# Three of the four mLSTM heads' output projections as Strassen's seven products, spread over the next head

## The chip, the cores and the metric

The kernel runs on one core of a Trainium2 chip. A core has five engines that run side by side and wait for one another by semaphores: TensorE (PE in the profile; PEld is its loading of the stationary operand) multiplies into the eight banks of PSUM, VectorE (DVE) and ScalarE (ACT) work elementwise on SBUF and PSUM, GpSimd (POOL) does small work and issues some DMAs, SyncE (SP) issues the loads of the weights. Each engine takes its instructions in the order of the program. The metric is the device time of one execution in microseconds.

## The reference, cut to what matters

Two layers on a sequence of 512 tokens of width 1024. Each layer is a feed-forward, a mixer, a second feed-forward and a gated embedding. The first layer's mixer is an mLSTM with four heads; its last step takes the four heads' outputs, each 512 tokens by 512, side by side and multiplies them by `ml_w_out` (2048 by 1024):

```python
proj = x @ w_in + b_in                      # q, k: 256 columns a head; v, z: 512 a head
qk = jax.nn.silu(causal_depthwise_conv(qk, conv_w))
h = mlstm_cell(q, k, v, ig, fg)             # scores, mixing, normalisation by den
h = (h - mu) * lax.rsqrt(var + LN_EPS) * norm_g
h = (h * jax.nn.sigmoid(z)).astype(x.dtype)
return h @ w_out                            # a sum over heads of h_head @ w_out[512 rows]
```

Around it stands `x = layer_norm(ALPHA * x + mix)`. So each head's 512 by 512 output times its 512 rows of `w_out` is added into the residual x.

## The kernel before, in words

**Products.** Every matmul is done three times (`mm3`): an operand is split into a high part `hi` and a low part `lo = a - hi`, and hi·hi, hi·lo and lo·hi are added up in one PSUM bank. High parts are ScalarE copies (line 193 for weights, 273 for activations), low parts VectorE subtractions (199, 274). For some weights (`low="dma"`, lines 194 to 197) ScalarE writes the negated copy and a DMA issued by POOL adds the raw weight to it.

**Weights.** `Weights` holds one list, `W.order`, of all weight tiles of the program in the order of their use. `fill` goes down this list: it loads raw tiles through SP (three buffers of 1 MB) and splits one tile whenever a split buffer of the tile's kind is free; in the mLSTM four are "main" and two "extra". `take` hands TensorE the next split tile; `release` frees its buffer and at once calls `fill`, whose copies stand in the queues of ScalarE and VectorE at that point of the program. A release with `later=True` is kept back until `refill`. So a released tile is followed by the filling of the tile six places further on, and that fill waits until TensorE has used the released one.

**Strassen in the feed-forwards.** `forms` (line 92) gives, for four 2x2 blocks of a weight, the seven weight forms of Strassen's product (the variant with shared sums); the third and the fourth (`t2`, `t1`) need two VectorE additions each, made in place in the raw tiles. Low parts of forms are always made by VectorE (`in_place`). `Group` (line 719) does the other side: `form` makes the next of seven activation forms (VectorE additions before the third, fifth and sixth, then a split), `product` multiplies it into a pair of PSUM banks, `add` adds the result of the last product into x, two 512-column VectorE adds (`residual`). The products use two pairs of banks in turn, and most accumulate on what the pair holds, so a product must wait until the add of the product two before it has read that pair. The four banks, all of "dn", are pinned from the first two products until the adds of the last two.

**PSUM.** Four "up" banks go round in a fixed order. The four "dn" banks go by `dn_order`: `dn_bank` takes the first that isn't pinned and puts it at the end.

**The mLSTM, head by head.** `project_qk` projects two q and two k blocks (24 matmuls of 512 columns each, "qps"); after each, ScalarE copies the bank to `pad` (946), VectorE does the four taps of the convolution (948, 950), and one block later ScalarE and VectorE apply the silu and split it. `project_v` does four blocks of tokens ("vps"), each split after a VectorE add (981). `scores` does four triangular blocks ("sps"); `project_z` two blocks ("zps": sigmoid on ScalarE, a scale on VectorE); `mix` the four blocks of tokens from the last to the first ("nps", with statistics on VectorE, 1049 to 1061); then two more z blocks. Then `down` multiplies the output of the head *before* by its rows of `w_out` ("dps": 4 token blocks, 4 row blocks, 2 halves), and `gate_turn` turns this head's output by transposes ("hps"), gates it and splits it into hh and hl. After the last head its own `down` follows, with the layer norm. In the last head the transposes lie between the token blocks of `down`.

The order of all of this is written out by hand in the order of the calls.

Of the kernel before, what the change touches and what calls it, by code (L numbers as in the profile page):

```python
# [9 lines left out]
F32 = mybir.dt.float32  # L10
# [36 lines left out]
class Weights:  # L47
# [179 lines left out]
                self.free[kind] += 1  # L227
            self.fill(low=low)

    def refill(self, n=1):  # L230
        for kind in self.held[:n]:
            self.free[kind] += 1
        del self.held[:n]
        self.fill()


@with_exitstack
def hybrid_trunk(ctx: ExitStack, tc, x, p, ln_g, ln_b, ffn1_wgu, ffn1_wd, ffn2_wgu, ffn2_wd,
# [93 lines left out]
    def ffn_weights(wgu, wd, name, ple=False):  # L332
# [26 lines left out]
            W.add_hook("rows", lambda hi, lo: turn_p.pop()(hi, lo))  # L359
        add_rows(wd, starts[LAST], 4, ["rows", "rows", "main", "main"] if ple else ["main", "rows", "rows", "rows"])  # L360

    def stage_kinds(first):

        n = len(W.order) - first
        for i in range(n):
            extra = i % 6 >= 4 if i < n // 6 * 6 else i >= n - 2
            W.order[first + i] = ("extra" if extra else "main",) + W.order[first + i][1:]

    def ml_weights():
        win, wout = ml_w_in[0], ml_w_out[0]  # L370
        first = len(W.order)

        def o_w(h):
            add_rows(wout, 4 * h, 4)

        for h in range(HEADS):
            W.add((w_cols(win, h * DQK), cols2))
# [10 lines left out]
        for i, kind in zip(range(-8, -4), ("extra", "extra", "main", "main")):  # L388
            W.order[i] = (kind,) + W.order[i][1:]

    def gm_weights():
# [211 lines left out]
        if norm.deferred:  # L603
            affine.extend([lambda t=t: norm.finish(t) for t in range(TB)])

    def down(hs, first, norm=None, low=(None,) * 4, between=None, lazy=False, defer=False):


        n = len(hs)
# [2 lines left out]
        def release(k):  # L612
            kind = "rows" if kinds[k] == "rows" else None
            if norm is None:
                W.release(kind=kind, low=low[k])
            elif kind == "rows":
                W.free[kind] += 1
            elif defer:
                W.release()
            else:  # L620
                W.release(later=lazy or bool(W.held))
                if not W.held:
                    W.held.append("none")

        for t in range(TB):
# [26 lines left out]
            def finish(t=t, banks=banks):  # L652
                for half, ps in enumerate(banks):
                    residual(t, half, ps, first)
                    if norm is not None:
                        norm.stats(t, half, 2)
                if between is not None:
                    between(t)
# [60 lines left out]
    class Group:  # L719
# [56 lines left out]

    def ffn(layer, k, rows, prepare=None):
# [60 lines left out]

    def mlstm():
        b_in = ml_b_in  # L840
        with stage_pool("extra", EXTRA) as extra, stage_pool("ml_parts") as near, stage_pool("ml") as mp:
            W.open("extra", extra, EXTRA)
            rows_d = dram.tile([HEADS, SEQ], F32, name="rows_d")

# [83 lines left out]
            def project_qk(h):  # L928

                qh, ql = big("A", F32R, "qh"), big("B", F32R, "ql")  # L930

# [9 lines left out]
                for i in range(4):  # L941
# [26 lines left out]
                late()  # L968
                return qh, ql

            def project_v(h, vb, between=()):
# [5 lines left out]
                for t in range(TB):  # L977
                    ps = dn_bank("vps")
                    up_tokens(t, ws, ps, release=lambda: None)
# [4 lines left out]
                    if t < len(between) and between[t]:  # L984
                        between[t]()
                return vh, vl

            def project_z(h, sz, i):

                ps = up_bank("zps")  # L990
                up(ps, W.take())
                sca.activation(sz[:, i], ps, AF.Sigmoid, bias=col("b_z", h * 4 + i))
                vec.tensor_scalar(sz[:, i], sz[:, i], col("norm_g", h * 4 + i), None, op0=OP.mult)
                W.release(later=i < 2, low="dma")
                run_affine()

            def row_tile():
                return mp.tile([P, SEQ], F32, name="rbc", tag="rbc")
# [5 lines left out]
            def scores(h, qk, rt):  # L1004
# [2 lines left out]
                res = []  # L1007
                for j in range(TB):
                    n = SEQ - j * P
                    ps = (dn_bank if j % 2 else up_bank)("sps")  # L1010
# [15 lines left out]
                    res.append((sh, sl))  # L1026
                return res

            def mix(h, ss, v):
                vh, vl = v  # L1030
                hn = big("A", F32, "hn")
                for t in reversed(range(TB)):
                    bank = up_bank if t >= 2 else dn_bank
# [30 lines left out]

            def gate_turn(h, hn, sz):

                if h < HEADS - 1:
                    hh, hl = big("hh", F32R, "hh"), big("hl", F32R, "hl")
                else:

                    hh, hl = (near.tile([P, 4, SEQ], F32R, name=n, tag=g) for n, g in (("hh", "vh"), ("hl", "vl")))

                def turn(t):
                    ps = (dn_bank if t % 2 and h < HEADS - 1 else up_bank)("hps").rearrange("p (k c) -> p k c", k=4)
# [3 lines left out]
                    hf = tmp_tile("hzf").rearrange("p (k c) -> p k c", k=4)  # L1078
                    vec.tensor_mul(hf, ps, sz[:, :, s])
                    split(hh[:, :, s], hl[:, :, s], hf)  # L1080
                return [(hh[:, i], hl[:, i]) for i in range(4)], turn

            prev = None
            for h in range(HEADS):
                vb = mp.tile([P, DV], F32, name="vb", tag="sh0")
                sca.dma_start(vb, row_ap(b_in, 2 * QK + h * DV, DV))
                if h:
                    rt = row_tile()
                    load_row(rt, h)
                qk = project_qk(h)  # L1090
                if h == 0:
                    rt = row_tile()
                    v = project_v(h, vb, (None, lambda: (gate_sums(), run_affine()),
                                          lambda: (gate_rows(), load_row(rt, h), run_affine())))
                else:
                    v = project_v(h, vb)
                W.release()
                ss = scores(h, qk, rt)
                sz = big("B", F32, "sz")
                W.release()  # L1100
                W.release(2, later=True)
                for i in range(2):
                    project_z(h, sz, i)
                hn = mix(h, ss, v)
                W.refill(4)
                for i in range(2, 4):
                    project_z(h, sz, i)
                last = h == HEADS - 1
                if last:
                    hs, turn = gate_turn(h, hn, sz)  # L1110
                if prev is not None:
                    down(prev, h == 1, low=[None, None, "dma", "dma"] if last else ["dma"] * 4,
                         between=turn if last else None)
                else:
                    norm = Norm(0, 1)
                if not last:
# [297 lines left out]
```

## Time and profile before

| | |
|---|---|
| median of 3 runs | 2244.51 us (2244.25 to 2244.77) |
| the profiled execution | 2244.37 us, its span 2242.7 us |
| TensorE busy | 2228.5 us, 99% |
| VectorE, ScalarE, POOL busy | 1482.4, 902.0, 102.8 us |
| TensorE's granted clock, mean | 0.999 |
| matmuls of 128x512 in the mLSTM's `down` (dps<-hh) | 384, of them 96 a head |

The span runs from the first to the last instruction. A matmul's row shows its whole passage (some 390 ns), while the next one starts after 227 to 233 ns; so the pace is read from starts. Numbers in brackets at the end of a timeline row are the idle time of the engine before it and what ended it. The mLSTM stands from about 362 to 776 us, its heads start at about 362, 449, 550 and 650.

### The profile page before, as it was taken

How to read it: one execution, taken by the hardware profiler on the slowest of the kernel's cores; microseconds unless marked ns; L12 is line 12 of the kernel's file. 1: busy time of each engine (PE TensorE's matmuls, PEld its weight loads, DVE VectorE, ACT ScalarE, POOL GpSimd, SP SyncE). 2: the span in 40 equal slices, each digit the busy share in tenths (PEclk: the TensorE clock that was granted, in tenths of full speed). 3: DMA queues.
4: the chain of work that ended last, by engine and by line, in shares of the span. 5: the costliest groups of instructions: out<-in, count | busy, mean ns of one | idle time of the engine just before them, and what ended most of it. 6: DMA issues, size and time to landing. Idle time of an engine off the chain costs nothing.

```text
span 2242.7 us, 26516 instructions
## 1 busy us (share of the span) xinstructions
PE 2228.5 (99%) x10625; PEld 1869.4 (83%) x10625; DVE 1482.4 (66%) x2179; ACT 902.0 (40%) x1281; POOL 102.8 (5%) x136
## 2 busy tenths in 40 slices
PE   9999999999999999999999999999999999999998
PEld 8888888888888888888889888888888888888887
DVE  5666667755555676666687766666666578666677
ACT  4333336454545443333345333334243453333332
POOL 1000001111111000000000000000010100000000
PEclk9999999999999999999999999999999999999999
DMA  7322223376684543331233422323355443332221
GB/s 236 126 92 85 94 86 107 79 172 127 146 161 101 152 132 118 100 111 63 98 122 108 133 95 89 94 85 99 117 141 141 103 151 122 123 113 85 85 85 56
DMA packets 201970, 254.07 MB, mean 113 GB/s; under 512 B 5828, under 2 KB 155460, under 8 KB 201848
## 3 DMA queue, kind: packets, MB, share of 16 engines
q1 hardware_dynamic: 168080, 211.83, 29.3%
q0 software_dynamic: 27152, 25.87, 7.9%
q10 hardware_dynamic: 6616, 14.69, 2.0%
q8 instruction: 83, 1.36, 0.2%
q14 instruction: 39, 0.32, 0.0%
HBM read 224.58 MB, written 2.11 MB: 101 GB/s over the span
## 4 chain that ended last, share of the span: by engine, by line
PE 97%; issue 1%; ACT 1%; DMA 1%; DVE 1%; SPq 0%; POOL 0%; DVEq 0%; POOLq 0%; ACTq 0%
PE fps L268 13%; PE fps L269 13%; PE fps L270 13%; PE gps L270 6%; PE gps L268 6%; PE gps L269 6%; PE dps L268 4%; PE dps L270 4%; PE dps L269 4%; PE gups L268 1%; PE zps L268 1%; PE gups L269 1%; PE gvps L270 1%; PE zps L270 1%; PE gups L270 1%; PE gvps L268 1%
## 5 line engine op out<-in xcount | busy, mean ns | idle before, releaser
L268 PE MATMUL fps<-xh,whi 128*128 128x512 f32 x1312 | 510.7, 389 | 0.0
L269 PE MATMUL fps<-xl,whi 128*128 128x512 f32 x1312 | 510.4, 389 | 0.0
L270 PE MATMUL fps<-xh,wlo 128*128 128x512 f32 x1312 | 510.4, 389 | 0.0
L199 DVE TENSOR_TENSOR wlo<-wraw,whi 128x1024 fp32r<-128x1024 f32 (+1 forms) x276 | 332.6, 1218 | 138.2 <-ACT whi L193 137.0
L193 ACT ACTIVATE whi<-wraw 128x1024 fp32r<-128x1024 f32 (+1 forms) x325 | 336.5, 1048 | 195.8 <-PE fps L269 81.3
L199 DVE TENSOR_TENSOR wlo<-wquarter,whi 128x1024 fp32r<-128x1024 f32 (+1 forms) x140 | 156.6, 1118 | 218.1 <-ACT whi L193 218.1
L270 PEld LDWEIGHTS fps<-xh,wlo 128*128 128x128 f32 x1312 | 246.3, 188 | 51.3
L268 PEld LDWEIGHTS fps<-xh,whi 128*128 128x128 f32 x1312 | 246.3, 188 | 50.9
L269 PEld LDWEIGHTS fps<-xl,whi 128*128 128x128 f32 x1312 | 246.3, 188 | 50.8
L193 ACT ACTIVATE whi<-wquarter 128x1024 fp32r<-128x1024 f32 (+1 forms) x140 | 136.3, 974 | 280.0 <-PE gps L270 208.9
L270 PE MATMUL gps<-whi,flo 128*128 128x512 f32 x504 | 196.1, 389 | 0.0
L268 PE MATMUL gps<-whi,fhi 128*128 128x512 f32 x504 | 196.1, 389 | 0.0
L269 PE MATMUL gps<-wlo,fhi 128*128 128x512 f32 x504 | 196.1, 389 | 0.0
L580 DVE TENSOR_TENSOR xt<-xt,gps 128x512 f32<-128x512 f32 x248 | 158.6, 681 | 0.0
L806 ACT ACTIVATE sg<-fps 128x512 f32<-128x512 f32 x80 | 48.0, 600 | 228.1 <-PE fps L270 228.1
L273 ACT ACTIVATE fhi<-h 128x512 fp32r<-128x512 f32 (+1 forms) x140 | 80.6, 582 | 143.1 <-DVE h L744 54.4
L274 DVE TENSOR_TENSOR flo<-h,fhi 128x512 fp32r<-128x512 f32 (+1 forms) x140 | 87.2, 635 | 42.9 <-ACT fhi L273 42.9
L270 PEld LDWEIGHTS gps<-whi,flo 128*128 128x128 f32 x504 | 94.6, 188 | 19.7
L269 PEld LDWEIGHTS gps<-wlo,fhi 128*128 128x128 f32 x504 | 94.6, 188 | 19.6
L268 PEld LDWEIGHTS gps<-whi,fhi 128*128 128x128 f32 x504 | 94.6, 188 | 19.6
L268 PE MATMUL dps<-whi,hh 128*128 128x512 f32 x256 | 101.4, 396 | 0.0
L269 PE MATMUL dps<-wlo,hh 128*128 128x512 f32 x256 | 100.5, 393 | 0.0
(278 smaller groups left out, 3764.7 us busy)
## 6 DMA issues: line engine op xcount, KB each, us to landing
wraw<-in_ffn_wgu_dram SPq DMA_DIRECT2D x79, 1024.0 KB, 6.3
wquarter<-in_ffn_wd_dram SPq DMA_DIRECT2D x64, 512.0 KB, 3.7
wlo<-wraw POOLq DMA_DIRECT2D x49, 512.0 KB, 7.2
wraw<-in_ml_w_in_dram SPq DMA_DIRECT2D x24, 1024.0 KB, 5.6
wraw<-in_gm_w_in_dram SPq DMA_DIRECT2D x15, 1024.0 KB, 5.5
wraw<-in_ffn_wgu_dram SPq DMA_DIRECT2D x17, 512.0 KB, 4.2
wraw<-in_ffn_wd_dram SPq DMA_DIRECT2D x8, 1024.0 KB, 4.9
wraw<-in_ml_w_out_dram SPq DMA_DIRECT2D x8, 1024.0 KB, 5.5
```

What stands on the lines that cost most here:

```text
L193: self.nc.scalar.activation(hi[:, s], src[:, s], AF.Copy)
L199: self.nc.vector.tensor_sub(lo[:, s], src[:, s], hi[:, s].bitcast(F32))
L268: mm(ps, st[0], mv[0], start=start, stop=False, skip_group_check=more)
L269: mm(ps, st[0], mv[1], start=False, stop=False, skip_group_check=more)
L270: mm(ps, st[1], mv[0], start=False, stop=stop, skip_group_check=more)
L273: sca.activation(hi, src, AF.Copy)
L274: vec.tensor_sub(lo, src, hi.bitcast(F32))
L580: vec.tensor_add(dst, dst, ps)
L806: sca.activation(sg, ps, AF.Silu)
```

## The change

For heads 0 to 2 `down` is gone. Their four row blocks by 512 tokens go as one `Group` of seven products in the next head: two after the k blocks, four after the quarters of v, one after the last z block. Their weight forms stand in `W.order` behind tiles 2 to 7 and 11 of the twelve tiles of that head (`ML_SLOTS`). `w_out`'s rows of a head are loaded as two raw tiles, the second into the place of the layer norm's rows ("gb"), which is why `Norm(0, 1)` is now made just before the last head's `down`. The gated output of a head stays unsplit in `hf`; `Group.form` splits it.

For heads 1 to 3 `project_v` runs over the quarters of the contraction outside and the token blocks inside, in four up banks, and releases each weight tile; the scores take up banks only; the first z block takes a dn bank, since two are free after the sixth product's add; the third z block comes before the last step of `mix`. The releases of z's tiles and of v's last are put at other places. In the last head the seventh product lies between the second and the third transpose, and `down` has no transposes in it any more.

`unpin` sends a freed bank to the end of `dn_order`, where before it kept its place; this holds in the feed-forwards too.

```diff
-    def refill(self, n=1):
+    def refill(self, n=1, low=None):
...
+    def unpin(bank):
+        i = pinned.pop(id(bank))
+        dn_order.remove(i)
+        dn_order.append(i)
...
+    ML_SLOTS = (2, 3, 4, 5, 6, 7, 11)
...
             if h:
-                o_w(h - 1)
-        o_w(HEADS - 1)
+                tiles = W.order[at:]
+                del W.order[at:]
+                k = 4 * h - 4
+                j0, j1 = W.add_load(kp(wout)[:, k:k + 2, :], 3), W.add_load(kp(wout)[:, k + 2:k + 4, :], 3, "gb")
+                left, right = ((slice(None), slice(None), slice(c, c + 512)) for c in (0, 512))
+                down_w = W.forms("", (j0, left), (j0, right), (j1, right), (j1, left))
+                for i, tile_i in enumerate(tiles):
+                    W.order.append(tile_i)
+                    if i in ML_SLOTS:
+                        W.order.append(down_w[ML_SLOTS.index(i)])
+        add_rows(wout, 4 * HEADS - 4, 4)
...
                 if r >= 5:
-                    del pinned[id(ps)]
+                    unpin(ps)
...
                     W.release(low="dma")
+                    if i > 1:
+                        step()
...
+                banks = [up_bank("vps") for _ in range(TB)]
+                for k in range(4):
+                    w = W.take()
+                    if k == 3:
+                        group.add()
+                    for t, ps in enumerate(banks):
+                        for kb in (2 * k, 2 * k + 1):
+                            mm3(ps, xs(kb, t * P, (t + 1) * P), [a[:, kb % 2] for a in w], kb == 0, kb == KB - 1)
+                        if k == 3:
+                            take(t, ps)
+                    W.release(later=k == 3, low="dma")
+                    step(k == 3)
...
-                ps = up_bank("zps")
+                ps = (dn_bank if h and i == 0 else up_bank)("zps")
...
-                W.release(later=i < 2, low="dma")
-                run_affine()
+                W.release(later=h == 0 or i > 1)
+                if h == 0:
+                    run_affine()
...
+                    if t == 0:
+                        between()
+                    bank = dn_bank if t == 1 else up_bank
...
+            def step(later=False):
+
+                if group is not None:
+                    group.add()
+                    group.product()
+                    W.release(later=later, low="dma")
+                    group.form()
...
+                    v = project_v(h, vb, step)
+                    group.add()
...
+                hn = mix(h, ss, v, lambda: project_z(h, sz, 2))
+                if h == 0:
+                    W.open_raw("gb", act, 1)
+                W.refill(4 if h == 0 else 1)
+                project_z(h, sz, 3)
+                if h < HEADS - 1:
+                    step(True)
+                    if group is not None:
+                        group.add()
                     hs, turn = gate_turn(h, hn, sz)
                     for t in range(TB):
                         turn(t)
-                prev = hs
-            down(prev, False, norm)
+                    group = Group(hs, fpool, h == 0)
+                    group.form()
+                    group.form()
+                    W.refill(4, "dma")
+            hs, turn = gate_turn(h, hn, sz)
+            for t in range(TB):
+                turn(t)
+                if t == 1:
+                    step(True)
+                    group.add()
+            W.refill(4)
+            norm = Norm(0, 1)
+            down(hs, False, norm)
```

## Rows read from the trace of the kernel before

**Rows 1.** The cores' spans and clock; the page's first part (busy, share, instructions).
```profile
core 0: 2242.7 us, clock 0.999
...
PE 2228.5 (99%) x10625; PEld 1869.4 (83%) x10625; DVE 1482.4 (66%) x2179; ACT 902.0 (40%) x1281; POOL 102.8 (5%) x136
```

**Rows 2.** TensorE's waits: in total, times, the longest, in us.
```profile
PE dps L268 <- DVE xt L580: 2.3, 2, 1.1
...
PE vps L269 <- DMA wlo<-wraw: 0.2, 1, 0.2
```

**Rows 3.** Timeline of TensorE, the third head: start us, us, engine, line, operation.
```profile
549.90 0.48 PE L268 MATMUL qps<-xh,whi 128*128 128x512 f32 x1
...
571.79 0.39 PE L268 MATMUL vps<-whi,xh 128*128 128x512 f32 x1
...
593.59 0.39 PE L268 MATMUL sps<-qh 128*128 128x512 f32 x1
...
597.35 0.45 PE L268 MATMUL zps<-xh,whi 128*128 128x512 f32 x1
...
608.30 0.28 PE L1039 MATMUL nps<-vh,sh 128*128 128x258 f32 x1
...
615.49 0.39 PE L268 MATMUL zps<-xh,whi 128*128 128x512 f32 x1
...
626.39 0.39 PE L268 MATMUL dps<-whi,hh 128*128 128x512 f32 x1
...
648.79 1.47 PE L1076 MATMUL hps<-ident,hn 128*128 128x128 f32 x12
```

**Rows 4.** Timeline of TensorE, one product in the third feed-forward stage.
```profile
858.97 0.39 PE L268 MATMUL gps<-whi,fhi 128*128 128x512 f32 x1
...
861.69 0.39 PE L268 MATMUL fps<-xh,whi 128*128 128x512 f32 x1
```

**Rows 5.** Timeline of VectorE, weight and activation forms in the first feed-forward.
```profile
83.75 1.22 DVE L105 TENSOR_TENSOR wquarter<-wquarter 128x1024 f32<-128x1024 f32 x1
...
88.58 1.28 DVE L578 SCALAR_TENSOR_TENSOR xt<-xt,gps 128x512 f32<-128x512 f32 x2
...
99.36 0.68 DVE L743 TENSOR_TENSOR h<-h 128x512 f32<-128x512 f32 x1
...
102.14 1.28 DVE L580 TENSOR_TENSOR xt<-xt,gps 128x512 f32<-128x512 f32 x2
```

**Rows 6.** Timeline of VectorE, convolutions and v blocks of the third head.
```profile
560.57 0.49 DVE L948 TENSOR_SCALAR acc<-pad,cols 128x512 f32<-128x512 f32 x1 [1.41 <-ACT pad L946]
...
563.55 0.49 DVE L948 TENSOR_SCALAR acc<-pad,cols 128x512 f32<-128x512 f32 x1
...
566.96 0.06 DVE L945 MEMSET pad<- 128x3 f32 x1
...
584.06 0.68 DVE L981 TENSOR_TENSOR vf<-vps,vb 128x512 f32<-128x512 f32 x1
...
585.90 0.68 DVE L981 TENSOR_TENSOR vf<-vps,vb 128x512 f32<-128x512 f32 x1
```

**Rows 7.** Timelines of ScalarE (two rows) and VectorE, z blocks and mixing, third head.
```profile
608.50 0.69 ACT L992 ACTIVATE sz<-zps,cols 128x512 f32<-128x512 f32 x1 [0.83 <-PE zps L270]
609.08 3.89 ACT L193 ACTIVATE whi<-wraw 128x1024 fp32r<-128x1024 f32 x4
...
605.69 1.23 DVE L199 TENSOR_TENSOR wlo<-wraw,whi 128x1024 fp32r<-128x1024 f32 x1 [0.66 <-ACT whi L193]
...
611.01 0.43 DVE L1049 BATCH_NORM_STATS2 hst<-nps 128x6 f32<-128x256 f32 x1 [1.30 <-PE nps L1041]
...
613.66 0.99 DVE L1061 TENSOR_SCALAR hn<-nps,hmv,hr 128x256 f32<-128x256 f32 x2
```

**Rows 8.** Timelines of VectorE and TensorE, start of a feed-forward's last down.
```profile
1105.15 1.28 DVE L580 TENSOR_TENSOR xt<-xt,gps 128x512 f32<-128x512 f32 x2
...
1105.98 0.47 PE L268 MATMUL dps<-whi,wquarter 128*128 128x512 f32 x1 [1.13 <-DVE xt L580]
```

More of the change, by code (lines that the diff above doesn't have):

```diff
@@ L233, in refill @@
         del self.held[:n]
-        self.fill()
+        self.fill(low=low)
 @with_exitstack
@@ L371, in ml_weights @@
         first = len(W.order)
[L373 to L374 removed]
         for h in range(HEADS):
+            at = len(W.order)
             W.add((w_cols(win, h * DQK), cols2))
@@ L604, in set_hooks, with down @@
             affine.extend([lambda t=t: norm.finish(t) for t in range(TB)])
-    def down(hs, first, norm=None, low=(None,) * 4, between=None, lazy=False, defer=False):
+    def down(hs, first, norm=None, lazy=False, defer=False):
         n = len(hs)
@@ L614, in release @@
             if norm is None:
-                W.release(kind=kind, low=low[k])
+                W.release(kind=kind)
             elif kind == "rows":
@@ L840, in mlstm @@
         b_in = ml_b_in
-        with stage_pool("extra", EXTRA) as extra, stage_pool("ml_parts") as near, stage_pool("ml") as mp:
+        with stage_pool("extra", EXTRA) as extra, stage_pool("ml_parts") as near, stage_pool("forms", 2) as fpool, \
+                stage_pool("ml") as mp:
             W.open("extra", extra, EXTRA)
@@ L969, in project_qk, with project_v @@
                 return qh, ql
-            def project_v(h, vb, between=()):
+            def project_v(h, vb, step, between=()):
                 ws = []
@@ L976, in project_v, with take @@
                 vec.memset(vh[:, :, HV:HV + 2].bitcast(F32), 1.0)
-                for t in range(TB):
-                    ps = dn_bank("vps")
-                    up_tokens(t, ws, ps, release=lambda: None)
+                def take(t, ps):
                     vf = tmp_tile("vf")
@@ L1009, in scores @@
                     n = SEQ - j * P
-                    ps = (dn_bank if j % 2 else up_bank)("sps")
+                    ps = (dn_bank if j % 2 and h == 0 else up_bank)("sps")
                     s = slice(j * P, (j + 1) * P)
@@ L1027, in scores, with mix @@
                 return res
-            def mix(h, ss, v):
+            def mix(h, ss, v, between):
                 vh, vl = v
@@ L1065, in gate_turn @@
             def gate_turn(h, hn, sz):
-                if h < HEADS - 1:
-                    hh, hl = big("hh", F32R, "hh"), big("hl", F32R, "hl")
+                last = h == HEADS - 1
+                if last:
+                    hh, hl = (near.tile([P, 4, SEQ], F32R, name=n, tag=g) for n, g in (("hh", "vh"), ("hl", "vl")))
                 else:
-                    hh, hl = (near.tile([P, 4, SEQ], F32R, name=n, tag=g) for n, g in (("hh", "vh"), ("hl", "vl")))
+                    hf = mp.tile([P, 4, SEQ], F32, name="hf", tag="hf")
                 def turn(t):
-                    ps = (dn_bank if t % 2 and h < HEADS - 1 else up_bank)("hps").rearrange("p (k c) -> p k c", k=4)
+                    ps = (up_bank if last or t % 2 == 0 else dn_bank)("hps").rearrange("p (k c) -> p k c", k=4)
                     for i in range(4):
@@ L1077, in turn @@
                     s = slice(t * P, (t + 1) * P)
[L1078 to L1083, printed above, removed]
+                    if not last:
+                        vec.tensor_mul(hf[:, :, s], ps, sz[:, :, s])
+                        return
+                    f = tmp_tile("hzf").rearrange("p (k c) -> p k c", k=4)
+                    vec.tensor_mul(f, ps, sz[:, :, s])
+                    split(hh[:, :, s], hl[:, :, s], f)
+                return [(hh[:, i], hl[:, i]) for i in range(4)] if last else hf, turn
+            group = None
+            def step(later=False):
[4 more added lines that the diff above has]
+                    group.form()
             for h in range(HEADS):
@@ L1089, in mlstm @@
                     load_row(rt, h)
-                qk = project_qk(h)
+                qk = project_qk(h, step)
                 if h == 0:
                     rt = row_tile()
-                    v = project_v(h, vb, (None, lambda: (gate_sums(), run_affine()),
-                                          lambda: (gate_rows(), load_row(rt, h), run_affine())))
-                else:
-                    v = project_v(h, vb)
-                W.release()
+                    v = project_v(h, vb, step, (None, lambda: (gate_sums(), run_affine()),
+                                                lambda: (gate_rows(), load_row(rt, h), run_affine())))
+                    W.release()
+                else:
+                    v = project_v(h, vb, step)
+                    group.add()
                 ss = scores(h, qk, rt)
                 sz = big("B", F32, "sz")
-                W.release()
-                W.release(2, later=True)
+                if h == 0:
+                    W.release()
+                    W.release(2, later=True)
+                else:
+                    W.refill(2)
                 for i in range(2):
                     project_z(h, sz, i)
[L1104 to L1116, printed above, removed]
+                hn = mix(h, ss, v, lambda: project_z(h, sz, 2))
+                if h == 0:
+                    W.open_raw("gb", act, 1)
[5 more added lines that the diff above has]
+                        group.add()
                     hs, turn = gate_turn(h, hn, sz)
```

16 lines of the change are left out of this document (9 added, 7 removed).

## The prediction

> **What bounds the kernel now.** [...] Then the waits of TensorE by line: apart from the start they come to 2.5 us, and 2.3 of them are one wait that happens twice, for a VectorE add that empties a PSUM bank [rows 2]. The reader is to see that nothing else is late: VectorE (66% busy) and ScalarE (40%) hold TensorE up in no other place. Then the timeline of TensorE over one head [rows 3]: four projections for q and k take 21.89 us (549.90 to 571.79), v 21.80, the scores 3.76, two z blocks 10.95, the mixing 7.19, two z blocks 10.90, the down projection of the head before 22.40 (626.39 to 648.79), then the transposes. The blocks follow each other without a hole. So there is no slack in TensorE to win back in this stage except by issuing fewer matmuls, and none in the order of the work if another engine is late once.
>
> The profiled execution took 2244.37 us, 1.67 more than its span and 0.14 less than the median of the runs, 2244.51. I add to 2244.37.
>
> **What goes.** A down projection is 4 token blocks x 4 row blocks x 2 halves x 3 = 96 matmuls of 512 columns; seven products are 7 x 2 x 2 x 3 = 84. The 96 took 22.40 us, 0.2333 each [rows 3]. The same twelve-matmul product stands in the feed-forward stage: 858.97 to 861.69, 2.72 us, 0.2267 each [rows 4]. I take 7 x 2.72 = 19.04 there too (the bound is 84 x 0.2333 = 19.60). That is 3.36 us less for each of three heads: **-10.1 us** (-8.4 at the bound).
>
> The second gain is the order of freed banks. The last chunk of a feed-forward takes its first banks from the front of the line; those were the even products', which the seventh product's add empties last. That is the wait of 1.13 us at 1105.98 and its twin [rows 2, 8]. With freed banks sent to the end, the odd products' banks come first, empty since the add before. What is late next: the split weights, which VectorE finished before it came to that add at 1105.15, and the last hidden block, which only the fourth row block needs, three half products (4.1 us) later; both are there. **-2.3 us** (bounds 0 and -2.3). The 0.2 us for a low half that a DMA makes [rows 2] goes too, as that fill now has more time: **-0.2**.
>
> **What comes.** None of the added work is on TensorE; the question is whether VectorE, in program order, is in time. Per head it gets 4 additions of 1024-element weight forms, 4 additions on the 512-element activations, three more low halves of activations, six more residual adds, and about three more low halves of weights, which in the kernel before a DMA made. At 1.2 us for 1024 elements and 0.64 to 0.69 for 512 that is some 17 us in a head of 100 (549.90 to 648.79 and the transposes), on top of a mean of 66%. As a mean it fits. It does not fit at one place.
>
> *The third product.* It writes the banks of the first one, so it must wait for the first one's add. That add is queued on VectorE behind the convolution of the last k block. I count from the head's start. TensorE ends q's second block at 10.95 (half of 21.89). ScalarE's copy comes 0.20 later and takes 0.69, as at 608.50 [rows 7], so VectorE starts this block's convolution at 11.85. Then in order:
> - convolution and the low half of the block before: 563.55 to 566.96, 3.41 [rows 6], to 15.26;
> - the third weight form, filled where q's second tile was: two additions, the wait for ScalarE's high half, the low half, 83.75 to 88.58, 4.83 [rows 5], to 20.09;
> - the next convolution and low half, 3.41 and 0.06 for a memset, to 23.56;
> - the fourth weight form, again 4.83, to 28.39;
> - the third activation form, 99.36 to 102.14, 2.78 [rows 5], to 31.17;
> - the last convolution and low half, 3.47, to 34.64;
> - the first of the two residual adds, half of 1.28, to 35.28, and 0.15 until TensorE starts (the first of the two adds from 1105.15 lasts to about 1105.83, TensorE starts at 1105.98 [rows 8]): 35.4.
>
> TensorE is there at 21.89 + 2 x 2.72 + a quarter of 21.80 = 32.78. So it waits 2.7 us. VectorE is never idle in this chain but for ScalarE, whose copies are included, so nothing in it gives way. In the three heads: 8.1. The head after the first starts later still: four weight splits stand on VectorE between its last normalisation and the turned blocks, then two splits of the first forms, then on ScalarE a weight fill and two DMA issues, and by the same count its second convolution starts 1.1 late (bounds 0 and 2.1). **+9.2 us** (bounds 7 and 13).
>
> *The first z block* takes a bank that the sixth product's add frees. From the end of the fifth product: 0.2, a z tile's two copies on ScalarE (two of the four in 3.89 [rows 7], 1.9), the last activation form's split (a little under half of 2.78, 1.3), two adds 1.28, four v blocks at 1.84 (584.06 to 585.90 [rows 6]) 7.36, one add 0.64, 0.15: 12.8. TensorE comes after a quarter of v, a product and the scores, 5.45 + 2.72 + 3.76 = 11.9. Wait 0.9 a head: **+2.7** (0 to 4.5).
>
> *The third z block* now comes ahead of the last mixing step, 0.9 of 7.19 = 6.5 us after the mixing starts, and takes the first bank that the mixing filled. Before, the statistics of that bank started 2.7 us after the mixing did (611.01, VectorE idle 1.30 until TensorE was done), and the bank was read 3.2 us after that (613.66 and 0.54) [rows 7]: at 5.9. Now the release of z's second block puts a k tile's split ahead of the statistics. It starts after the sigmoid (0.2 + 0.69, and it is pushed to 1.8 by the fill of the tile before), then 1.0 for the high half and 1.23 for the low one [rows 7]: statistics at 4.0, bank free at 7.3. Wait 0.9 a head: **+2.7** (0 to 4).
>
> *The last head's down* no longer alternates with its turned blocks: its first matmul needs the first block turned and split, which stands on VectorE behind three weight splits of 1.2. One product and four transposes cover part: **+1.3** (0 to 3.6).
>
> Loads cost nothing: each weight is asked for some six tiles ahead, and the load into the place of the norm's rows has from the fill of a head's last form (after the scores) to that of the next head's second form (after the transposes), which is two z blocks, the mixing and two more: 29 us [rows 3]. SP and POOL get fewer, later-needed issues. If that cover were gone, one load would show as a wait of some us in a v block.
>
> **Sum.** -10.1 - 2.3 - 0.2 + 9.2 + 2.7 + 2.7 + 1.3 = +3.3: 2244.37 + 3.3 = **2247.7 us**, 0.14% more. About 0.2% (4.5 us) is what a measurement of this kernel can tell from no change, so I forecast no change. By the ends of the terms that are likely together it is 2244 to 2250.
>
> [...] TensorE's clock is 0.999 over the span, and the two waits of 1.13 us left it there [rows 1, 8]. No row shows a wait of 2.7 us in the middle of the kernel. [...]
>
> **The rivals.**
> 1. *VectorE starts every head in debt* (slower). In heads three and four I count the first convolution from 7.1 to 9.9 (ScalarE copies a k tile twice and a form once and issues two DMAs ahead of it), so VectorE is free 2 us before the second. Before, the first convolution of a head started 10.67 us in (560.57 against 549.90 [rows 3, 6]), behind ScalarE's fills. If it does so again, the second starts at about 13.5, not 11.85, in each head: +1.6 twice, +0.5 in the second head, +3.7 in all, **2251.4**. It decides once the first convolution starts later than 9 us in. For it: the ScalarE queue at the head's end still has a fill by DMA, a form and two issues; against: fewer fills stand there now.
> 2. *The third product's wait covers the rest.* TensorE, once late, gives VectorE time; if the small waits (2.7 + 2.7 + 1.3) go, the time is **2241.0**. For it: each is the difference of two long sums; against: I counted them from after the wait.
> 3. *VectorE keeps up*, as it does in the feed-forward stage, where the same forms never hold TensorE: 2244.37 - 12.6 = **2231.8**. Against it: there 24-matmul blocks without convolutions lie between the products.
> [...]
>
> **How the numbers follow.** Forecast 0.42, rival 1 0.24, rival 2 0.19, rival 3 0.11, rival 4 0.04. About half of rival 2 (0.09) lies below 2240.0, with rival 3 that is 0.20 for faster. Of the forecast some 0.07 lies above 2249.0, and of rival 1 all but 0.02: with rival 4 0.33 for slower. That leaves 0.47 within 0.2%. The range that leaves out rivals 3 and 4 and the edges is 2238 to 2255; it takes in the bounds of the unknown costs but for all of one sign at once. The forecast's own range is 2244 to 2250.
>
> **What would show it.** Right: seven product blocks a head at about 2.72 us with 84 matmuls; a TensorE wait of 2 to 4 us on a residual add ahead of the third product in each of three heads, the longest in the second; under 1 us ahead of the first and third z blocks; no wait on a residual add at the feed-forwards' last chunk. Wrong: no wait ahead of the third product (then rival 3), a wait on a weight or a load there instead, a granted clock under 1.00, or a waiting sum of TensorE far from 16 us.

## The result and the profile after

The changed kernel takes 2249.86 us (median of 12 runs, 2248.85 to 2252.01) against 2244.71 of the kernel before (12 runs, 2244.25 to 2245.18): ratio 1.0024, 95% interval 1.0017 to 1.0032. It is slower, by 5.2 us. The profiled execution took 2249.62 us. Its cores' view:

```profile
core 0: 2247.9 us, clock 0.998
```

TensorE has fewer instructions and less busy time than in [rows 1], the first part of the page says, so what was lost was lost in waits:

```profile
PE 2224.6 (99%) x10589; PEld 1864.4 (83%) x10589; DVE 1529.6 (68%) x2242; ACT 913.2 (41%) x1296; POOL 100.7 (4%) x133
```

TensorE's waits (in total, times, the longest, in us). The pair of [rows 2] at the feed-forwards is gone; 11.7 us in 9 waits of the mLSTM stage stand there instead, and one of 0.3 after it:

```profile
PE gps L268 <- DVE xt L593: 4.7, 2, 2.3
PE gps L268 <- DVE xt L591: 2.4, 1, 2.4
PE xps L461 <- DVE xt L570: 1.8, 1, 1.8
PE zps L268 <- DVE xt L593: 1.6, 3, 0.6
...
PE zps L268 <- DVE hn L1097: 1.2, 2, 0.6
...
PE gvps L269 <- DVE wlo L199: 0.3, 1, 0.3
```

The timeline of TensorE in the third head, beside [rows 3, 4]. The head starts at 551.45; its first product runs from 567.91 to the next block's matmul at 570.70, 2.79 us and not 2.72; the third product starts after 2.34 us of nothing:

```profile
551.45 0.48 PE L268 MATMUL qps<-xh,whi 128*128 128x512 f32 x1
...
567.91 0.39 PE L268 MATMUL gps<-whi,fhi 128*128 128x512 f32 x1
...
570.70 0.39 PE L268 MATMUL qps<-xh,whi 128*128 128x512 f32 x1
...
586.90 0.50 PE L268 MATMUL gps<-whi,fhi 128*128 128x512 f32 x1 [2.34 <-DVE xt L593]
587.24 0.40 PE L269 MATMUL gps<-wlo,fhi 128*128 128x512 f32 x1
```

What it waited for is on VectorE's timeline, the same head. Read it from the second convolution (563.38) down: from there VectorE only ever waits for ScalarE's copies, and the add that frees the bank (586.16) is the last in the row:

```profile
557.94 0.49 DVE L960 TENSOR_SCALAR acc<-pad,cols 128x512 f32<-128x512 f32 x1 [0.77 <-ACT pad L958]
...
563.38 0.49 DVE L960 TENSOR_SCALAR acc<-pad,cols 128x512 f32<-128x512 f32 x1 [2.58 <-ACT pad L958]
...
570.36 1.23 DVE L199 TENSOR_TENSOR wlo<-wraw,whi 128x1024 fp32r<-128x1024 f32 x1 [1.12 <-ACT whi L193]
...
578.74 1.23 DVE L199 TENSOR_TENSOR wlo<-wraw,whi 128x1024 fp32r<-128x1024 f32 x1 [1.19 <-ACT whi L193]
...
581.99 0.69 DVE L274 TENSOR_TENSOR flo<-hf,fhi 128x512 fp32r<-128x512 f32 x1 [0.70 <-ACT fhi L273]
...
582.80 0.49 DVE L960 TENSOR_SCALAR acc<-pad,cols 128x512 f32<-128x512 f32 x1
...
586.16 1.28 DVE L593 TENSOR_TENSOR xt<-xt,gps 128x512 f32<-128x512 f32 x2
```

The last head's down is the second place; its first matmul starts at 754.80. On VectorE, its first residual add (765.18) stands behind the last two turned blocks and two low halves of weights, so the norm is applied only at 769.00:

```profile
757.38 1.28 DVE L593 TENSOR_TENSOR xt<-xt,gps 128x512 f32<-128x512 f32 x2
...
761.95 0.69 DVE L274 TENSOR_TENSOR hl<-hzf,hh 128x512 fp32r<-128x512 f32 x1 [0.70 <-ACT hh L273]
762.90 2.36 DVE L199 TENSOR_TENSOR wlo<-wraw,whi 128x1024 fp32r<-128x1024 f32 x2 [0.26 <-ACT whi L193]
765.18 0.68 DVE L593 TENSOR_TENSOR xt<-xt,dps 128x512 f32<-128x512 f32 x1
...
769.00 0.81 DVE L570 TENSOR_SCALAR xt<-xt,mv,rs 128x1024 f32<-128x1024 f32 x1 [0.66 <-POOL rs L563]
```

In the kernel before, the same add came 5.2 us after the start of that down:

```profile
751.46 0.48 PE L268 MATMUL dps<-whi,hh 128*128 128x512 f32 x1
...
756.63 0.69 DVE L580 TENSOR_TENSOR xt<-xt,dps 128x512 f32<-128x512 f32 x1 [1.53 <-PE dps L270]
```

On TensorE after the change the first transposes of x wait for it, and the matmuls behind them run 0.43 apart instead of 0.23:

```profile
767.80 0.39 PE L270 MATMUL dps<-whi,hl 128*128 128x512 f32 x1
769.96 0.98 PE L461 MATMUL xps<-ident,xt 128*128 128x128 f32 x4 [1.77 <-DVE xt L570]
...
771.17 0.63 PE L269 MATMUL dps<-wlo,hh 128*128 128x512 f32 x1
771.60 0.63 PE L270 MATMUL dps<-whi,hl 128*128 128x512 f32 x1
```

That is the clock. Windows of the same stretch; the granted clock is the third column from the right, 0.50 between two stretches at 1.00:

```profile
755.00:767.00 12.00, 12.00 (x51) 9.21 (x50) 9.61 (x14) 3.80 (x5) 0.00 (x0) 1.00 0.58 184
770.10:773.50 3.40, 3.40 (x11) 2.72 (x11) 2.91 (x7) 2.14 (x5) 0.53 (x1) 0.50 0.65 210
773.50:783.00 9.50, 9.50 (x49) 7.83 (x48) 6.29 (x12) 6.42 (x16) 0.56 (x2) 1.00 0.00 0
```

### The profile page after: what moved, and what is told of

Read it like the earlier page. It is cut to its first block, busy times and chain, and to the rows that moved or that the text cites. A ratio compares the mean times of both kernels' runs of the same rounds, so it can differ in the third digit from the quotient of the medians.

```text
span 2247.9 us, 26543 instructions
## 1 busy us (share of the span) xinstructions
PE 2224.6 (99%) x10589; PEld 1864.4 (83%) x10589; DVE 1529.6 (68%) x2242; ACT 913.2 (41%) x1296; POOL 100.7 (4%) x133
## 4 chain that ended last, share of the span: by engine, by line
PE 87%; DVE 7%; ACT 4%; issue 1%; POOL 0%; DMA 0%; ACTq 0%; DVEq 0%; POOLq 0%
PE fps L268 13%; PE fps L270 13%; PE fps L269 13%; PE gps L268 7%; PE gps L270 7%; PE gps L269 7%; PE dps L269 3%; PE dps L270 3%; PE dps L268 3%; DVE wlo L199 1%; PE gups L268 1%; PE gups L269 1%; PE gups L270 1%; PE xps L461 1%; DVE acc L962 1%
## 5 line engine op out<-in xcount | busy, mean ns | idle before, releaser
L199 DVE TENSOR_TENSOR wlo<-wraw,whi 128x1024 fp32r<-128x1024 f32 (+1 forms) x288 | 347.7, 1218 | 149.3 <-ACT whi L193 147.8
L268 PE MATMUL gps<-whi,fhi 128*128 128x512 f32 x588 | 229.6, 390 | 7.1 <-DVE xt L593 4.7
L270 PE MATMUL gps<-whi,flo 128*128 128x512 f32 x588 | 229.3, 390 | 0.0
L269 PE MATMUL gps<-wlo,fhi 128*128 128x512 f32 x588 | 229.2, 390 | 0.0
L593 DVE TENSOR_TENSOR xt<-xt,gps 128x512 f32<-128x512 f32 x282 | 180.4, 681 | 0.9 <-PE gps L270 0.9
L268 PEld LDWEIGHTS gps<-whi,fhi 128*128 128x128 f32 x588 | 110.4, 188 | 31.5 <-DVE xt L593 5.5
L269 PEld LDWEIGHTS gps<-wlo,fhi 128*128 128x128 f32 x588 | 110.4, 188 | 23.4
L270 PEld LDWEIGHTS gps<-whi,flo 128*128 128x128 f32 x588 | 110.4, 188 | 23.4
L563 POOL TENSOR_TENSOR rs<-rs,eps_pow 128x1 f32<-128x1 f32 x32 | 20.6, 644 | 1575.5 <-DVE rs L562 1575.5
L466 ACT ACTIVATE xf<-xps,cols 128x128 f32<-128x128 f32 x160 | 59.9, 454 | 55.7 <-PE xps L461 55.6
```

What stands on the lines that cost most here:

```text
L199: self.nc.vector.tensor_sub(lo[:, s], src[:, s], hi[:, s].bitcast(F32))
L268: mm(ps, st[0], mv[0], start=start, stop=False, skip_group_check=more)
L269: mm(ps, st[0], mv[1], start=False, stop=False, skip_group_check=more)
L270: mm(ps, st[1], mv[0], start=False, stop=stop, skip_group_check=more)
L466: sca.activation(xf[:, k], ps[:, k], AF.Identity, scale=col("ln_g", norm.at + 4 * g + k), bias=col("ln_b", norm.at + 4 * g + k))
L593: vec.tensor_add(dst, dst, ps)
```

## The experiments

Times are medians; each ratio is to the kernel before on the same chip (2244.63 to 2244.74).

**The order of freed banks alone**, put into the kernel before (label e3_banks_alone):

```diff
+    def unpin(bank):
+        i = pinned.pop(id(bank))
+        dn_order.remove(i)
+        dn_order.append(i)
...
-                    del pinned[id(ps)]
+                    unpin(ps)
```

> The kernel before with one part of the change alone: freed banks go to the end of the line. Theory: the two waits of 1.13 us ahead of the last down of two feed-forwards go, nothing takes their place, and the time falls by 2.3 to 2.6 us, to 2242.2. Rival (the split weights or the last hidden block are late there by as much): under 1 us is won.

2241.35 us, ratio 0.9985 (0.9976 to 0.9994), and no wait of TensorE on an add is left. The part is worth its 2.3 to 2.6 and a little more (3.3). In its trace the wait for a low half that a DMA makes [rows 2] is gone too, though no weight fill was changed.

**The first product's add ahead of the last convolution** (e1_add_first), in the changed kernel:

```diff
                     ps = banks.popleft() if banks else project()
+                    if group is not None and i == 3:
+                        group.add()
```

> The add of the first product is issued ahead of the last k block's convolution instead of behind it; nothing else changes. Theory (the add stands in VectorE's queue behind that convolution and low half, 3.5 us): the wait of 2.4 us ahead of the third product falls under 0.2 in all three heads, the time falls by some 7.5 us from 2249.9 to 2242.4, and the waits ahead of the first and third z blocks (0.5 and 0.6) stay, since they are counted from after it. Rival (the third product would be held by its own activation form or weight form, ready at about the same time): a wait of 1 to 2 us stays there and ends with ScalarE's or VectorE's split; 2245 to 2248. Rival (VectorE's debt is only handed on): the wait turns up ahead of a later product or z block, time above 2247.

2239.54 us, 10.3 less than the change, ratio 0.9977 (0.9967 to 0.9986): this one line turns the loss into a gain. All three waits ahead of the third product are gone. The forecast was 7.5 less. In its profile the clock did not fall behind the transposes' wait (0.999 over the span; a fall costs some 1.6 us), and the wait at 1595 us is gone (0.5). The others stayed:

```profile
PE xps L461 <- DVE xt L570: 1.8, 1, 1.8
PE zps L268 <- DVE xt L593: 1.7, 3, 0.6
...
PE zps L268 <- DVE hn L1099: 1.2, 2, 0.6
```

**The last down's two low halves by DMA** (e2_low_by_dma):

```diff
-            W.refill(4)
+            W.refill(4, "dma")
             norm = Norm(0, 1)
```

> The two weight tiles filled just before the last head's down get their low halves by a DMA instead of by VectorE (2.36 us less in its queue). Theory (the transposes of the new x wait 1.8 us for the normalisation because VectorE reaches the first residual add of that down 5 us later than before): the residual add comes at about 762.8 instead of 765.2, the wait is gone, the granted clock stays 1.00 there (it was 0.76 from 767 to 773, matmuls 427 ns apart), and the time falls by 1.9 + 1.2 to 1.7, about 3.3 us, to 2246.5. Rival (the lower clock has nothing to do with the wait): the clock falls in the same place, and only 1.9 us are won, 2248. Rival (VectorE's four turned blocks alone make it late): a wait of 1 us or more stays.

2247.44 us, 2.4 less than the change, ratio 1.0011 (1.0002 to 1.0020). The wait of the transposes fell from 1.77 to 0.51, and the clock stayed at 1.00 behind it; in this execution it fell behind the wait of the last head's third product (2.3 us) instead (0.998 over the span).

**Three fills in other places** (e5_z_places): the activation form ahead of the fill behind each product, and the fill behind a head's second z block after the third:

```diff
-                W.release(later=h == 0 or i > 1)
+                W.release(later=h == 0 or i > 0)
...
                     group.product()
-                    W.release(later=later, low="dma")
                     group.form()
+                    W.release(later=later, low="dma")
...
-                W.refill(4 if h == 0 else 1)
+                W.refill(4 if h == 0 else 2)
```

> Only the places of three fills change: the next activation form is split ahead of the release behind each product (so the z tile's low half no longer stands ahead of it on VectorE), and the release behind a head's second z block is put off until after the third, so that no weight split stands ahead of the mixing's statistics. Theory (small waits from VectorE's order, lengths add): the waits ahead of the first z block (0.57, 0.57 and 0.66 us over one matmul's pace in the three heads) and ahead of the third (0.67 twice) go, 3.1 us: 2249.9 - 3.1 = about 2246.7, the waits of 2.4 us ahead of each third product stay as they are. Rival (the small waits only take up what the third product's wait or the turned blocks would otherwise wait, rival 2 of the prediction turned round): the waits go and the next one grows by as much, time within 1 us of 2249.9.

The five waits ahead of z blocks are gone from the trace, but the time is 2248.18 us, 1.7 less and not 3.1; ratio 1.0015 (1.0006 to 1.0023). Where the rest went: in its profile the clock fell to 0.50 behind all three waits of a third product, three falls where the change's profile has one (mean clock 0.996 against 0.998). TensorE's timeline at the first of them; the pace goes from 0.23 to 0.43:

```profile
484.78 0.50 PE L268 MATMUL gps<-whi,fhi 128*128 128x512 f32 x1 [2.48 <-DVE xt L591]
485.12 0.40 PE L269 MATMUL gps<-wlo,fhi 128*128 128x512 f32 x1
485.35 0.40 PE L270 MATMUL gps<-whi,flo 128*128 128x512 f32 x1
...
486.39 0.63 PE L270 MATMUL gps<-whi,flo 128*128 128x512 f32 x1
486.82 0.63 PE L268 MATMUL gps<-whi,fhi 128*128 128x512 f32 x1
```

**Why a product takes 2.79 us and not 2.72.** The changed kernel allocates the activation forms, which are the products' stationary tiles, at byte 131232 of an SBUF partition, 32 past a multiple of 64; in the feed-forward they lie at 106624, a multiple of 128. First guess, multiples of 64 (e4_aligned): 32 more bytes for v.

```diff
-                vh = near.tile([P, TB, DV + 2], F32R, name="vh", tag="vh")
+                vh = near.tile([P, TB * (DV + 2) + 8], F32R, name="vh", tag="vh")
+                vh = vh[:, :TB * (DV + 2)].rearrange("p (t c) -> p t c", t=TB)
```

> The changed kernel with one tile (v's high part, 514 columns a block) made 32 bytes longer, so that all tiles laid out behind it, the activation forms among them, start 32 bytes further, at multiples of 64 bytes as they do in the feed-forward stages. Theory (the products' matmuls in this stage run 233 ns apart and not 227 because their stationary operand starts at an odd multiple of 32 bytes): all 252 of them run at 227 ns, 2.72 us a product instead of 2.79, and 1.5 us is won, or a little more with the last down (its low part lies behind the tile too): 2247.9 to 2248.4. Rival (it is the traffic of this stage, DMA or VectorE): 2.79 us a product as before, no change.

2250.45 us, products at 0.2332 a matmul: the guess fell. Second guess, the height in SBUF (e7_forms_low), the forms at 98432:

```diff
-        with stage_pool("extra", EXTRA) as extra, stage_pool("ml_parts") as near, stage_pool("forms", 2) as fpool, \
+        with stage_pool("extra", EXTRA) as extra, stage_pool("forms", 2) as fpool, stage_pool("ml_parts") as near, \
```

> The change as it is, with one pair of pools opened in the other order: the 256-column activation forms, which are the products' stationary tiles, lie 32 KB lower in SBUF (from byte 98432 instead of 131232 of a partition); q, k and v lie 8 KB higher. In the traces of before and after, all matmuls whose stationary tiles lie above byte 131072 (the down projections' hh and hl at 144544 and 152736, the forms at 131232 to 139424) run 0.2330 to 0.2340 apart, and those with stationary tiles below it 0.2265 to 0.2275. Theory (the place of the stationary tile in SBUF sets the pace): products 2.72 us instead of 2.79, 3 x 7 x 0.075 = 1.6 us less: about 2248.3. Rival (what runs beside the products in this stage sets it): pace stays at 0.2328, time 2249.9.

The pace is 0.2267, 2.72 us a product, so here the place decides and what runs beside it does not. The median hardly moved (2249.57; ratio 1.0021, 1.0012 to 1.0030). A faster TensorE waits longer for the same add, 2.52 to 2.55 us instead of 2.34 to 2.40, but that takes back only 0.5 of the 1.6 us. The profiled execution, with one fall of the clock like the change's, is 1.8 us faster (2247.80). Over all executions eight of eleven have a mean clock of 0.997 or less, against six of twelve of the change, so more falls probably took the rest; that is argued, not shown. But 98432 is also a multiple of 128, and the first guess had put the forms 64 past one. Two kernels tell height and multiple apart; both stand on the version with all four edits, below. One puts 32 empty bytes below the low forms (e10_off_by_32):

```diff
-        with stage_pool("extra", EXTRA) as extra, stage_pool("forms", 2) as fpool, stage_pool("ml_parts") as near, \
+        with stage_pool("extra", EXTRA) as extra, stage_pool("shift") as shift, stage_pool("forms", 2) as fpool, stage_pool("ml_parts") as near, \
...
+            shift.tile([P, 8], F32, name="shift")
```

> The version with all four edits, and 32 bytes of nothing allocated below the forms: they start at byte 98464 instead of 98432, q, k and v lie 32 bytes higher too. Theory (multiples of 128 bytes): the products go back from 0.2267 to about 0.2328 a matmul though they lie low, 252 x 0.0061 = 1.5 us more, and the scores (q's tiles are stationary there) get slower too, some 0.2 us in four heads: about 2234.1. Rival (the height): products stay at 0.2267, time 2232.4.

2234.07 us, 1.7 more than without the 32 bytes. The product that took 2.72 takes 2.79 again. A head's second product's start and the next block's, with the forms at 98432:

```profile
474.36 0.39 PE L268 MATMUL gps<-whi,fhi 128*128 128x512 f32 x1
...
477.08 0.39 PE L268 MATMUL vps<-whi,xh 128*128 128x512 f32 x1
```

and at 98464:

```profile
474.26 0.39 PE L268 MATMUL gps<-whi,fhi 128*128 128x512 f32 x1
...
477.05 0.39 PE L268 MATMUL vps<-whi,xh 128*128 128x512 f32 x1
```

The other half of its forecast fell. The scores, whose tiles of q and k moved to 32 past a multiple of 128 as well, were to lose 0.2 us in four heads; they take 3.76 us a head instead of 3.75 (3.78 in the first). Their start and the next block's, without the 32 bytes:

```profile
509.72 0.39 PE L268 MATMUL sps<-qh 128*128 128x512 f32 x1
...
513.47 0.45 PE L268 MATMUL zps<-xh,whi 128*128 128x512 f32 x1
```

and with them:

```profile
510.04 0.40 PE L268 MATMUL sps<-qh 128*128 128x512 f32 x1
...
513.80 0.46 PE L268 MATMUL zps<-xh,whi 128*128 128x512 f32 x1
```

So here the start of the stationary tile alone doesn't decide. In the scores both operands lie in those tiles and moved together; in the products the moving weights stayed at multiples of 128. That the two starts must match would fit both; no run tests it.

The other kernel (e9_vl_first) brings the last head's hl from 131232 to 123008 and hh above 131072:

```diff
-                vh = near.tile([P, TB, DV + 2], F32R, name="vh", tag="vh")
                 vl = near.tile([P, TB, DV], F32R, name="vl", tag="vl")
+                vh = near.tile([P, TB, DV + 2], F32R, name="vh", tag="vh")
```

> The version with all four edits, and v's low half allocated ahead of its high half. The forms stay at bytes 98432 to 106623 of a partition, a multiple of 128; the last head's hl, which had lain at 131232 (32 past a multiple of 128), comes to 123008 and its hh to 131200, both multiples of 128. Theory (a stationary tile whose start is no multiple of 128 bytes makes its matmuls slower; the earlier shift by 32 bytes had put the forms 64 past one): the last head's down goes from 0.2330 to 0.2270 a matmul, 96 x 0.006 = 0.6 us less: about 2231.8. Rival (it is the height: tiles above byte 131072 are slow): hh now lies above it, two of three matmuls have it as stationary tile, so the pace stays at 0.233 or more, time 2232.4.

The down's pace went from 0.2330 to 0.2284 on average, with hh high (131200): in these runs it is the offset from a multiple of 128, not the height. Twelve of its matmuls in a steady stretch, before this edit (2.80 us):

```profile
746.06 0.40 PE L268 MATMUL dps<-whi,hh 128*128 128x512 f32 x1
...
748.86 0.40 PE L268 MATMUL dps<-whi,hh 128*128 128x512 f32 x1
```

and with it (2.72 us):

```profile
746.23 0.39 PE L268 MATMUL dps<-whi,hh 128*128 128x512 f32 x1
...
748.95 0.39 PE L268 MATMUL dps<-whi,hh 128*128 128x512 f32 x1
```

The profile of the change had already spoken against the height: the last head's down has hh at 114816 and hl at 123040 there, both below 131072, and twelve of its matmuls take 2.80 us too (760.74 to 763.54). The time is 2232.03 (2231.71 to 2232.76, 5 runs), ratio 0.9944 (0.9931 to 0.9956), which can't be told from the version below; a wait of the transposes that grew from 0.5 to 0.8 took half of what the pace gave.

**All together**: the add, the DMA and the fills (e6_three), and the forms low as well (e8_four).

> The first product's add ahead of the last k block's convolution, the two low halves of the last down by DMA, and the new places of the three fills, all together. Theory (each removes its own wait and they add): from 2239.5 for the first alone, -1.2 for the last down and -3.1 for the z blocks: about 2235.2, TensorE's waits after the start together under 2 us, clock 1.00 throughout. Rival (moving the add ahead has used VectorE's slack, so that the other two only move the wait): 2238 to 2240 with a new wait in the q and k projections or in a v block.

2233.92 us, ratio 0.9951 (0.9939 to 0.9964). In its profile the clock does not fall before the kernel's last microseconds (0.998 over the span). The 1.3 us under the forecast are mostly the z blocks, whose waits had been counted short (see the table below).

> All together: the add ahead of the convolution, the low halves by DMA, the new places of the fills, and the forms low in SBUF. If the place of the stationary tile sets the pace: 1.6 us under the version without it, about 2233.6, products at 0.2267 a matmul. If not: the same as that version, about 2235.2.

2232.39 us (2232.01 to 2233.02, 5 runs), ratio 0.9944 (0.9931 to 0.9958), 12.3 less than before and 17.5 less than the change. Of TensorE's waits, this alone is over 0.2 us behind the start:

```profile
PE xps L461 <- DVE xt L570: 0.5, 1, 0.5
```

## Why the prediction was right or wrong

I forecast 2247.7 us and no change as the likeliest class; it is 2249.86, inside the forecast's own range of 2244 to 2250, and slower by 0.24%, just past the 0.2% that I had set (more than was needed: e3's 0.15% is clear of no change). The mechanism was the one forecast, but single terms missed by up to 2.8 us and partly cancelled; that the sum stayed in the range, 0.1 from its end, is in part luck. Forecast +3.3, measured +5.2 (of the spans), term by term from the profiled executions. A wait is taken from one matmul's start to the next, less the same step without a wait: 0.23 us between matmuls of 512 columns, 0.11 to 0.12 where, ahead of a z block, one of 128 or 256 columns comes first.

| term | predicted | measured |
|---|---|---|
| products | -10.1 (bound -8.4) | -8.5 |
| freed banks | -2.3 | -2.6 |
| low half by DMA | -0.2 | -0.4, and 0.5 for a new one at 1595 |
| third product | +9.2 | +7.6 |
| first z block | +2.7 | +2.1 |
| third z block | +2.7 | +1.55 |
| last head's down | +1.3 | +4.1 |
| first matmul after each of the eight waits on a residual add or a mixing bank: 0.31 to 0.34, without the wait 0.23 to 0.29 | none | +0.6 |

The measured terms sum to +4.95; the rest, some 0.25 us, has no place. The low half by DMA is not shown to be the change's doing, since e3 lost that wait as well.

- *Products.* I took the feed-forward's row [rows 4] where the stage's own row [rows 3] was the bound, and the stage's own was right: the same twelve matmuls take 2.79 or 2.72 us with their stationary tiles in one place or another. That is 1.6 us.
- *The third product* waits in all three heads, for the add that was named, behind the convolution that was named. From the second convolution the count gives 23.4 us to the add (11.85 to 35.28); the trace has 563.38 to 586.16 and half of 1.28, 23.4. The start was good to 0.1 (563.38 is 11.93 in), and TensorE started 35.45 in, 35.4 by the count. It came there 0.2 later than counted, for the two slower products. The first convolution starts 6.5 in, so rival 1 fell by its own condition (9 us). The second head's extra of 1.1 was nothing (its idle time is 2.40, the others' 2.34).
- *The z blocks* wait for what was named (a residual add, a mixing bank) but 0.7 to 0.8 a head each, not 0.9, and the last head's third not at all: there no fill stands in the way. Each was the difference of two sums of 7 to 13 us.
- *The last head's down* is the term that failed. I looked for the price at its first matmul; that one came in time (754.80, with 0.16 at the third). The price is at the first transposes of x, two token blocks on: the splits that the turned blocks and the fills queue on VectorE delay the first residual add to 10.4 us after the down's start, from 5.2 before. Of the 4.1 us, 2.5 is the wait with what surrounds it and 1.6 the clock. I followed the moved work to the first reader and not to the work queued behind it.
- *Rival 2* is right in its logic for single terms: a TensorE that arrives earlier waits longer (e7: products 1.6 us faster in sum, third waits 0.5 longer). As a forecast it fell: the small waits stayed, and e1 shows that they don't hang on the large ones (without these, the z waits were the same to 0.1).
- *Rival 3* is what the chip does once VectorE is in time: priced 2231.8, measured 2232.39 with four edits. So the gain that this rival counts can be had; the add in the wrong place hid 10.3 of the 17.5 us between the change and the best version, the other three edits the rest.
- *Rival 4*, a clock that falls behind the wait of every third product and stays low for a whole quarter of v (24 matmuls), was my estimate: none of the rows ahead of it shows such a fall, and no run shows that length. In e5 a fall comes behind all three of these waits, but each stays at 0.50 for some 3.3 us (in the first, eight matmuls). In the change's profiled execution the clock fell once ahead of the kernel's last microseconds (to 0.50, 770.10 to 773.50), behind the transposes' wait, and not behind the three longer ones. The changed kernel's six executions of 2248.85 to 2249.62 us have a mean clock of 0.998, five of 2250.1 to 2251.5 have 0.997, the one of 2252.01 has 0.996. A fall costs some 1.6 us (in e5, eight matmuls at 0.427 instead of 0.233). How many falls an execution has would then make the spread, 3.2 us where the kernel before has 0.9; this is argued from the mean clocks, for one execution alone was profiled. The clock went to 0.50 after gaps of 1.77 us in the change and 2.48 in e5. But behind 2.34 and 2.40 us in the change, and behind 1.76 in e1, it stayed at 1.00. What decides for one gap and not for the next isn't shown. So of the signs of being wrong that I named, a granted clock under 1.00 came, for one stretch; the waits of TensorE sum to 13 us, not 16.

## What to carry to other kernels

Where work of an off-path engine is put into the order by hand, follow each bank and each form to its last reader, and also ask what the moved work stands in front of; an operation that frees a bank for the bound engine goes ahead of operations that only feed the stage after. In these profiles a wait of some 2 us cost its length and sometimes a stretch at a clock of 0.50 behind it (1.6 us more); behind the two waits of 1.13 us in the kernel before it stayed at 1.00. Take a duration from the stage where the work will run, and when the same instruction has two paces in two stages (here 0.2267 and 0.233), compare where the tiles of both its operands begin.

## What the runs showed of the hardware

In these runs the pace of a 128x512 fp32r matmul went with where its tiles start in an SBUF partition. Where the moving tiles and the stationary ones start at multiples of 128 bytes, it is 0.2267 (forms at 98432 in e7 and e8, at 106624 in the feed-forward; x's at 49280 there, 33 matmuls in 7.48 us from 858.24 on in the change). With the stationary ones 32 past it is 0.2325 to 0.2333 (forms at 131232 in the change and at 98464 in e10, the old down's hh and hl at 144544 and 152736); 64 past 0.2332 (131264, e4). One stationary tile of the two was enough: in the last head's down of the change and of e8 hl alone stands 32 past, and twelve matmuls take 2.80 us, 0.2333 each. With both operands 32 past (the scores of e10) the scores take 3.76 us a head, against 3.75 with both at multiples of 128. Whether the two starts have to match isn't shown, since no run moved the moving tile alone; 96 past wasn't tried, and for 256-column matmuls no row was compared.
